# Time mixing: the next modulation tile's load is issued behind the present tile's instruction

## The chip, the cores and the metric

The kernel runs on one core of a Trainium2 chip. The metric is the device time of one execution in microseconds (us); lower is better. Before the change the median of three runs was 2669.53 us (2666.68 to 2670.61).

## What is computed

The reference is a two-layer encoder over 256 positions with 2048 channels. The first layer mixes along time with RWKV-7 recurrences for 32 heads, the second with chunked band attention; each layer ends in a squared-ReLU MLP. Cut to what matters here:

```
for layer in range(DEPTH):
    mod = c @ w_ada[layer] + b_ada[layer]
    sh1, sc1, gt1, sh2, sc2, gt2 = jnp.split(mod, 6, axis=-1)
    ...
    h = modulate(rms_norm(x, g_mix[layer]), sh1, sc1)
    y = rwkv7_time_mix(h, ...)          # layer 0; band attention in layer 1
    x = x + gt1[:, None, :] * y
    h = modulate(rms_norm(x, g_mlp[layer]), sh2, sc2)
    x = x + gt2[:, None, :] * sq_relu_mlp(h, w_up[layer], w_down[layer])
```

The **modulation** `mod` is a product of one row `c` with a matrix of 2048 x 12288 for each layer (and one of 2048 x 4096 for the shared keys and values). It has no use for TensorE's width, but all of its matrix must be read: it is cut into tiles of 128 x 1024, 384 of them behind the first two parts, 512 KB each. They are worked off in small steps beside the other work of the whole kernel.

## The kernel before

**Stages.** `layer_a` (L640) computes the first layer's projections up to v, and then the time mixing; `out_proj` (L929) follows, then the MLP, the attention, its `out_proj`, and the second MLP.

**The slots of the time mixing.** The heads are handled as 16 pairs. The loop at L896 runs over 8 x 16 + 36 = 164 slots. In each slot, every pair that is under way does one of its 36 steps (L907 to L910): `early` prepares its vectors, `invert` inverts a triangular matrix (on TensorE, L111, with VectorE's transposes L245 between), `late` runs the recurrence. A pair starts every 8 slots, the first at slot 8, with the matmuls L133 and L134. Behind these steps comes a slice of dense work (L921 to L923): in slots 0 to 127 two of the eight pieces of a projection (L860 to L870, `w_k` and `w_r` in turn, four slots each), afterwards pieces of the output projection `w_o` (`out_steps`, L872).

**Weights.** `weight` (L398) loads the two halves of a weight tile with `raw` (L366) and splits each in `halves` (L377): ScalarE casts it to wH (L384), VectorE subtracts to wL (L387). The load of the next projection's weight stands one projection ahead (`self.wnext`, L858). All loads are issued by SyncE (SP), in order, at L374 (parts of `w_o` at L395).

**Modulation.** `ada_tiles` (L433) lists the tiles, key by key, in two halves of sixteen. `ada_load` (L440) allocates a tile, issues its load and puts it in the queue `ada_q`. `ada_step` (L449) takes a tile from the queue, and calls `ada_load` first if the queue is empty; VectorE then adds the tile, times c, to `acc` (L460; the first of sixteen writes it, L458). Behind the sixteenth, `ada_sum` (L477) sums `acc` over the partitions with small matmuls (L482) and adds the bias (L486). `acc` has a single buffer, so the next sixteen begin when these matmuls have read it. `ada(n)` (L493) does n steps and then `ada_fill`, which loads ahead only where a stage has opened a pool of its own for these tiles (`ada_room`, tile `rada`). The time mixing has none: there `raw` takes the buffer from the six buffers of the tag `raw`, the same that the weights use. From slot 16 on, `self.ada()` is called in three slots of four (L924): 111 steps.

**What sets the order.** The code is traced in the order in which it stands; each engine's instructions are then ordered ahead of the run by a scheduler, which lets instructions that stand later go first where earlier ones are not ready. `issue_after(last)` keeps a block's matmuls behind the instruction `last` on TensorE. A load waits until the tile that had its buffer before has been read by its last reader.

**After the mixing.** `out_proj` loads x (L939), finishes the sums that `out_steps` began and, from n = 10 on, does one step for each tile that is still in the queue (`ada_drain`, L962). Today the queue is empty there.

Of the kernel before, what the change touches and what calls it, by code (L numbers as in the profile page):

```python
# [335 lines left out]
class Body:  # L336
# [303 lines left out]
    def layer_a(self, st, sp):  # L640
# [198 lines left out]
        with ExitStack() as s1:  # L839
            pw = self.pw = s1.enter_context(tc.tile_pool(name="pw", bufs=1, reuse_waits="tile"))  # L840
            pp = self.pp = sp.enter_context(tc.tile_pool(name="ps_b", bufs=1, space=bass.MemoryType.PSUM,
                                                         reuse_waits="tile"))
            self.psm = lambda: pp.tile([P, 512], F32, tag="ms", bufs=2, name="ms")
            self.bones = pw.tile([P, P], F32R, name="bones")
            nc.scalar.copy(self.bones, self.cst("bones"))
            e01 = [pw.tile([P, 4, C + 1], F32, name=f"e01_{i}") for i in range(2)]
            self.uf = [pw.tile([P, 4, C], F32, name=f"uf_{i}") for i in range(2)]
            for e, u in zip(e01, self.uf):
                nc.vector.memset(e[:, :, 0:1], 1.0)
                nc.gpsimd.memset(u, 0.0)  # L850

            pairs = [Pair(self, j, v[:, j, :], tw, ta, tg, e01[j % 2]) for j in range(NPAIR)]

            def proj_steps(pr):
                for dst, hl in (("k", xk), ("r", xr)):
                    w = self.wnext
                    src = next(weights, None)
                    self.wnext = None if src is None else self.weight(src)  # L858
                    ps = pp.tile([P, 2 * T], F32, tag="pj", bufs=2, name="pj")[:, :T]
                    for kt in range(KT):  # L860
                        self.proj(ps, w, lambda kt: hl[:, kt, :, 0:T], (kt, kt + 1))
                        if dst == "r" and kt == 1:
                            pr.lw = pw.tile([96, 2, P], F32, tag="lw", bufs=1, name="lw")
                            nc.sync.dma_start(out=pr.lw, in_=d["lora2"][pr.j, :96, 0:2])
                        if kt % 2 == 1:
                            if kt == KT - 1:
                                t = pw.tile([P, T], F32, tag=dst, bufs=2, name=dst)
                                nc.scalar.copy(t, ps)
                                setattr(pr, dst, t)
                            yield  # L870

            def out_steps():  # L872

                for n in range(8):
                    self.split(self.y_hl, n, v[:, n, :])
                sums, todo = self.o_ps, [(n, 0, HK) for n in range(8)] + [(n, HK, KT - 2) for n in range(4)]
                for n, lo, hi in todo:
                    if n % 2 == 0 and lo == 0:
                        tag = ("pj", "pj", "gr", "iv")[n // 2]
                        ps = pp.tile([P, 2 * T], F32, tag=tag, bufs=1 + (tag == "pj"), name="o")  # L880
                        sums.append(ps.rearrange("p (i t) -> p i t", i=2))
                    if lo == HK and n == 0:
                        assert all(p.done for p in pairs[:KT - 2])
                        for j in range(HK, KT - 2):
                            self.split(self.y_hl, j, v[:, j, :])
                    w = self.weight_part(d["w_o"][n], lo, hi)
                    for kt in range(lo, hi, 2):
                        self.proj(sums[n // 2][:, n % 2, :], w, lambda kt: self.y_hl[:, kt, :, 0:T],
                                  (kt, kt + 2), n % 2 == 0, False)
                        yield  # L890

            self.o_ps = []
            S, OUTS = self.SLOTS, 44
            inverts = range(Pair.EARLY, Pair.EARLY + Pair.INVERT)
            outs, done, n_out = None, 0, 0
            for slot in range(S * NPAIR + Pair.STEPS):  # L896
                live = []
                for j, pr in enumerate(pairs):
                    at = slot - S * (j + 1)
                    if 0 <= at < Pair.STEPS:  # L900
                        if at == 0:
                            pr.gen = pr.steps()
                        sums = at == Pair.STEPS - 3
                        live.append((0 if at in inverts else 1 + (at < Pair.EARLY) + 2 * sums, -at, pr))
                        pr.done = at == Pair.STEPS - 1
                last = self.last_pe()
                for _, _, pr in sorted(live, key=lambda x: x[:2]):  # L907
                    with tc.issue_after(last):
                        next(pr.gen)
                    last = self.last_pe()  # L910
                if slot < S * NPAIR:
                    if slot % S == 0:
                        dense = proj_steps(pairs[slot // S])
                    todo = 16 // S
                else:
                    if outs is None:
                        self.y_hl = self.new_hl()
                        outs = dense = out_steps()
                    todo = OUTS * (slot + 1 - S * NPAIR) // Pair.STEPS - n_out
                    n_out += todo  # L920
                with tc.issue_after(last):  # L921
                    for _ in range(todo):
                        next(dense, None)  # L923
                if slot >= 2 * S and slot % 4 < 3:  # L924
                    self.ada()
            self.fin(HK)
        return v

# [311 lines left out]
```

## Time and profile before

| | before |
|---|---|
| median of three runs | 2669.53 us (2666.68 to 2670.61) |
| profiled execution: its time | 2667.25 us |
| profiled execution: span | 2665.3 us |
| granted TensorE clock, mean | 0.992 |
| TensorE busy (matmul) | 2586.9 us, 97% |
| VectorE busy | 2104.5 us, 79% |
| ScalarE busy | 1369.2 us, 51% |
| moved by DMA | 662.69 MB, mean 249 GB/s |
| modulation loads: raw / rada from w_ada / rada from w_ada_kv | 111 / 209 / 64 |

How to read it: the span runs from the first to the last instruction of the core. PE is TensorE's matmuls and PEld its weight loads, which overlap; DVE is VectorE, ACT ScalarE, POOL GpSimd, SP SyncE, and a "q" behind an engine marks its sequencer (waits and issues of DMAs). A row of the timeline gives start, length, engine, line, operation, and the tile written and those read; in brackets the engine's idle time before it and what ended it. A row of waits gives the sum in us, how many times, and the longest. In rows by stretch, each engine's busy time is followed by its count of instructions.

### The profile page before, as it was taken

Reading aid. Unit: us, or ns where it says so; the run is one execution under the profiler, and the core shown is the slowest. Engines: PE = TensorE matmul, PEld = TensorE weight load, DVE = VectorE, ACT = ScalarE, POOL = GpSimd, SP = SyncE. Lnnn points to the kernel's source line nnn. Section 1 sums busy time; section 2 is a strip of 40 time slices with the busy share of each in tenths; the row PEclk is TensorE's granted clock in tenths of the full one; section 3 lists DMA queues with packets and bytes.
Section 4 is the critical chain, followed back from the end, with each engine's and each line's share of the span. In section 5 each row is a group of like instructions: output and inputs, shape, how many; then the busy total and the mean of one; then the engine's idle time right before and its main releaser. Section 6 shows DMA issues by size and latency. Waiting matters only on the chain.

```text
span 2665.3 us, 59286 instructions
## 1 busy us (share of the span) xinstructions
PE 2586.9 (97%) x24108; PEld 2258.5 (85%) x24108; DVE 2104.5 (79%) x3070; ACT 1369.2 (51%) x2516; POOL 210.2 (8%) x336
## 2 busy tenths in 40 slices
PE   7998999999999999999999999999999999999997
PEld 4788888888899888888888998877898888888886
DVE  6788888888889888888888898899887556556555
ACT  3345656556456345355365554565564464553554
POOL 0002323223100000000001100000100000000002
PEclk9999999999999999999999999999999999999999
DMA  9976656566768898889888779887766555555553
GB/s 353 313 243 205 202 183 201 182 202 199 252 235 308 309 324 323 318 328 335 319 328 292 231 248 322 320 274 256 267 215 237 185 188 189 184 188 190 189 190 119
DMA packets 207153, 662.69 MB, mean 249 GB/s; under 512 B 21408, under 2 KB 54560, under 8 KB 206880
## 3 DMA queue, kind: packets, MB, share of 16 engines
q1 hardware_dynamic: 204816, 656.36, 71.8%
q8 instruction: 189, 3.10, 0.5%
q10 hardware_dynamic: 2064, 2.54, 0.3%
q14 instruction: 84, 0.69, 0.1%
HBM read 656.72 MB, written 2.10 MB: 247 GB/s over the span
## 4 chain that ended last, share of the span: by engine, by line
PE 83%; DVE 7%; issue 3%; DMA 3%; ACT 2%; POOL 1%; DVEq 0%; ACTq 0%; SPq 0%; POOLq 0%
PE pj L418 41%; PE pj L419 21%; PE pj L407 3%; PE pj L408 3%; PE pj L409 3%; DVE wL L387 2%; DVE acc L460 2%; DMA raw<-w_ada 1%; PE iv L111 1%; DMA rada<-w_ada 1%; ACT wH L384 1%; PE o L407 1%; PE gr L105 1%; PE ms L330 1%; PE o L408 0%
## 5 line engine op out<-in xcount | busy, mean ns | idle before, releaser
L387 DVE TENSOR_TENSOR wL<-raw,wH 128x1024 fp32r<-128x1024 f32 x772 | 941.1, 1220 | 352.8 <-ACT wH L384 346.9
L384 ACT CAST wH<-raw 128x1024 fp32r<-128x1024 f32 x772 | 805.7, 1045 | 783.6 <-PE pj L418 594.6
L418 PE MATMUL pj<-aHL,wH 128*128 128x512 f32 x2816 | 998.1, 398 | 1.3 <-DVE x L953 1.3
L419 PE MATMUL pj<-aHL,wL 128*128 128x256 f32 x2816 | 791.4, 281 | 0.2 <-DVE wL L387 0.2
L418 PE MATMUL pj<-hHL,wH 128*128 128x512 f32 x2048 | 723.0, 398 | 0.0
L418 PEld LDWEIGHTS pj<-aHL,wH 128*128 128x128 f32 x2816 | 531.6, 189 | 129.4 <-issue 8.5
L419 PE MATMUL pj<-hHL,wL 128*128 128x256 f32 x2048 | 573.8, 280 | 0.3 <-DVE wL L387 0.3
L419 PEld LDWEIGHTS pj<-aHL,wL 128*128 128x128 f32 x2816 | 531.6, 189 | 1.8 <-issue 0.8
L418 PEld LDWEIGHTS pj<-hHL,wH 128*128 128x128 f32 x2048 | 384.7, 188 | 95.0 <-DVE hHL L999 0.2
L419 PEld LDWEIGHTS pj<-hHL,wL 128*128 128x128 f32 x2048 | 386.5, 189 | 0.8 <-DVE wL L387 0.6
L460 DVE SCALAR_TENSOR_TENSOR acc<-rada,ct,acc 128x1024 f32<-128x1024 f32 x256 | 328.2, 1282 | 11.1 <-DMA rada<-w_ada 10.1
L407 PE MATMUL pj<-aHL,wH 128*128 128x256 f32 (+1 forms) x896 | 263.3, 294 | 0.1
L408 PE MATMUL pj<-aHL,wH 128*128 128x256 f32 (+1 forms) x896 | 254.7, 284 | 0.0
L409 PE MATMUL pj<-aHL,wL 128*128 128x256 f32 (+1 forms) x896 | 253.5, 283 | 0.0
L524 POOL TENSOR_TENSOR ss<-ss,sq 128x256 f32<-128x256 f32 x56 | 54.1, 966 | 1588.2 <-ACT sq L523 1587.9
L407 PEld LDWEIGHTS pj<-aHL,wH 128*128 128x128 f32 x896 | 170.5, 190 | 5.1 <-issue 0.5
L409 PEld LDWEIGHTS pj<-aHL,wL 128*128 128x128 f32 x896 | 171.0, 191 | 0.2
L408 PEld LDWEIGHTS pj<-aHL,wH 128*128 128x128 f32 x896 | 170.6, 190 | 0.5
L1024 DVE SCALAR_TENSOR_TENSOR x<-pj,mod,x 128x256 f32<-128x256 f32 x256 | 123.4, 482 | 58.5 <-PE pj L419 54.9
L460 DVE SCALAR_TENSOR_TENSOR acc<-raw,ct,acc 128x1024 f32<-128x1024 f32 x104 | 139.9, 1345 | 12.9 <-DMA raw<-w_ada 12.3
L996 ACT ACTIVATE t<-t 128x256 f32<-128x256 f32 x112 | 46.8, 418 | 123.1 <-DVE t L968 123.1
L998 ACT ACTIVATE t<-t 128x256 f32<-128x256 f32 x128 | 53.4, 417 | 3.4
(250 smaller groups left out, 2825.3 us busy)
## 6 DMA issues: line engine op xcount, KB each, us to landing
raw<-w_up SPq DMA_DIRECT2D x256, 512.0 KB, 4.2
raw<-w_down SPq DMA_DIRECT2D x256, 512.0 KB, 4.3
rada<-w_ada SPq DMA_DIRECT2D x209, 512.0 KB, 5.8
raw<-w_ada SPq DMA_DIRECT2D x111, 512.0 KB, 4.4
rada<-w_ada_kv SPq DMA_DIRECT2D x64, 512.0 KB, 6.1
rawa<-w_ada SPq DMA_DIRECT2D x32, 512.0 KB, 6.8
rawa<-w_ada_t SPq DMA_DIRECT2D x32, 512.0 KB, 7.6
raw<-w_k SPq DMA_DIRECT2D x32, 512.0 KB, 3.9
```

Source lines behind the costliest of these rows:

```text
L384: nc.scalar.copy(Hf, raw)
L387: eng.tensor_tensor(out=Lf, in0=raw, in1=Hf, op=ALU.subtract)
L407: nc.tensor.matmul(ps, H[:, i, :], a(kt)[:, 0, :], start=(first and kt == 0), stop=False)
L408: nc.tensor.matmul(ps, H[:, i, :], a(kt)[:, 1, :], start=False, stop=False)
L409: ins = nc.tensor.matmul(ps, L[:, i, :], a(kt)[:, 0, :], start=False, stop=(last and kt == KT - 1))
L418: nc.tensor.matmul(ps, H[:, i, :], a(kt), start=(kt == 0), stop=False)
L419: ins = nc.tensor.matmul(ps[:, 0, :], L[:, i, :], a(kt)[:, 0, :], start=False, stop=(kt == KT - 1))
L460: nc.vector.scalar_tensor_tensor(out=self.acc, in0=raw, scalar=ck, in1=self.acc, op0=ALU.mult, op1=ALU.add)
L524: (eng or nc.gpsimd).tensor_tensor(out=self.ss, in0=self.ss, in1=sq, op=ALU.add)
L996: nc.scalar.activation(t, t, AF.Relu)
L998: nc.scalar.activation(t, t, AF.Square)
L1024: nc.vector.scalar_tensor_tensor(out=x, in0=ps[:, i, :], scalar=self.mods[(layer, 5)][:, n:n + 1], in1=x, op0=ALU.mult, op1=ALU.add)
```

## The change

In slots 16 and later with slot % 4 < 3 one step is still done. Behind it, and also in slot 15 and in every fourth slot, a tile is loaded if the queue is empty.

```
@@ -921,8 +921,11 @@
                 with tc.issue_after(last):
                     for _ in range(todo):
                         next(dense, None)
-                if slot >= 2 * S and slot % 4 < 3:
-                    self.ada()
+                if slot >= 2 * S - 1:
+                    if slot >= 2 * S and slot % 4 < 3:
+                        self.ada_step()
+                    if not self.ada_q:
+                        self.ada_load()
             self.fin(HK)
         return v
```

S is 8. The load of a step in slot 0, 1 or 2 of four then stands in the slot before, and for slot 0 two slots before, since the slot with remainder 3 does no step. The last step of the loop is that of slot 162; behind it the 112th tile is loaded, and its step is the first that `ada_drain` in `out_proj` finds.

## The prediction

> **What bounds the kernel now.** I read the page's head first, then busy time by stretch (the time mixing runs from 214 us, the first pair's matmul of L134, to 707 us, where the loads of x begin).
>
> ```profile
> span 2665.3 us, 59286 instructions
> ...
> PE 2586.9 (97%) x24108; PEld 2258.5 (85%) x24108; DVE 2104.5 (79%) x3070; ACT 1369.2 (51%) x2516; POOL 210.2 (8%) x336
> ```
> ```profile
> 214.00:707.00 493.00, 465.54 (x9965) 418.99 (x9964) 416.38 (x746) 278.99 (x787) 128.52 (x192) 0.99 0.63 200
> 707.00:760.00 53.00, 50.48 (x325) 46.34 (x324) 42.72 (x57) 29.95 (x49) 10.96 (x12) 0.97 0.86 287
> 760.00:2665.30 1905.30, 1888.28 (x12250) 1645.10 (x12249) 1482.51 (x1955) 973.80 (x1531) 55.90 (x111) 1.00 0.73 255
> ```
>
> The columns are PE, PEld, DVE, ACT and POOL, then clock, DMA share and GB/s. TensorE is the bound: outside the mixing it is idle for 17 us of 1905. In the mixing it is idle for 493.00 - 465.54 = 27.5 us; whatever the change can win there lies in these 27.5 us. VectorE is free for 493.00 - 416.38 = 76.6 us of the stage. Next, who TensorE waits for in that stretch, and everything that touches the tile "raw", which carries both the weights and the modulation:
>
> ```profile
> PE iv L111 <- DVE tt L245: 10.1, 11, 4.1
> ```
> ```profile
> L374 SPq DMA_DIRECT2D raw<-w_ada x111: 327/328/1397, 217.0 to 696.5; - x111
> L460 DVE SCALAR_TENSOR_TENSOR acc<-raw,ct,acc x104: 1236/1278/2173, 226.9 to 705.7; 128x1024 f32<-128x1024 f32 x104
> ...
>   PE pj L408: 43.6, 43
>   ACT wH L384: 15.5, 15
>   DMA raw<-w_ada: 12.3, 15
>   DMA raw<-w_o: 5.0, 2
> ```
>
> The largest wait of TensorE, 10.1 us, is on VectorE's transposes of the inversion. VectorE itself stands still for a modulation tile 15 times, 12.3 us in all; this is what the change aims at. The weights are early: the casts (wH, L384) wait for a matmul to free wH 43 times, never for a load of w_k or w_r, and for w_o twice (5.0 us).
>
> **When a load goes out today.** SP's queue and VectorE's releases of raw buffers, side by side (a row's x2 spans both issues, each 0.33 us long):
>
> ```profile
> 392.11 1.46 SPq L374 DMA_DIRECT2D raw<-w_k  x2
> 394.57 2.83 SPq L374 DMA_DIRECT2D raw<-w_ada  x2
> 398.67 0.33 SPq L864 DMA_DIRECT2D lw<-lora  x1
> 399.05 1.40 SPq L374 DMA_DIRECT2D raw<-w_ada  x1
> 402.71 2.31 SPq L374 DMA_DIRECT2D raw<-w_r  x2
> ```
> ```profile
> 390.79 1.28 DVE L460 SCALAR_TENSOR_TENSOR acc<-raw,ct,acc 128x1024 f32<-128x1024 f32 x1
> 392.00 1.22 DVE L387 TENSOR_TENSOR wL<-raw,wH 128x1024 fp32r<-128x1024 f32 x1
> 393.26 1.28 DVE L460 SCALAR_TENSOR_TENSOR acc<-raw,ct,acc 128x1024 f32<-128x1024 f32 x1
> 395.77 1.28 DVE L460 SCALAR_TENSOR_TENSOR acc<-raw,ct,acc 128x1024 f32<-128x1024 f32 x1
> ...
> 401.03 1.65 DVE L460 SCALAR_TENSOR_TENSOR acc<-raw,ct,acc 128x1024 f32<-128x1024 f32 x1 [1.48 <-DMA raw<-w_ada]
> ```
>
> The instruction at 390.79 ends at 392.07 and SP issues at 392.11; the next ends at 393.22, and the second w_k goes at 392.11 + 1.46 - 0.33 = 393.24; 394.54 is followed by 394.57, 397.05 by 397.07, 402.68 by 402.71. Each of these loads leaves within 0.04 us of a release. So all six raw buffers are always taken, and the hour of a load is set by the next buffer to come free, not by its place in the code. The step at 401.03 waits 1.48 us although SP issued its load the moment it could.
>
> How far do the steps already run ahead of their place in the code? Five rows: instructions of L460, of L458 and of L134 up to 401 us (the count stands behind the x), all of L134, and the last of L134 before it in the timeline.
>
> ```profile
> 200.00:401.00 201.00, 48.73 (x36) 0.98 0.63 198
> ```
> ```profile
> 200.00:401.00 201.00, 2.74 (x3) 0.98 0.63 198
> ```
> ```profile
> 200.00:401.00 201.00, 4.75 (x16) 3.04 (x16) 0.98 0.63 198
> ```
> ```profile
> L134 PE MATMUL ms<-ta,lw x32: 377/379/379, 214.3 to 627.0; 96*128 96x256 f32 x32
> ```
> ```profile
> 398.05 0.59 PE L134 MATMUL ms<-ta,lw 96*128 96x256 f32 x2
> ```
>
> Up to 401 us VectorE had begun 36 steps on L460 and 3 on L458 (the first of each sixteen), so the step at 401.03 is number 39, counted from 0. Three steps per four slots from slot 16 on put it at slot 16 + 4 x 13 = 68. L134 has two instructions for each pair: 32 of them, from 214.3 to 627.0, are 16 pairs in 412.7 us, so a pair's 8 slots take 412.7 / 15 = 27.5 us and a slot 3.44 us. The 16 up to 401 are eight pairs; the eighth begins in slot 64, at 398.05, and slot 68 comes at about 411.8. The step runs 11 us, three slots, before its place: it fills VectorE's gaps as soon as its tile has landed.
>
> **The change, part by part.** *The order of the loads.* Per four slots the old code asks SP for w, w, A, A, A, with each A (slots 0, 1, 2) just ahead of its own step. The new one asks in slot 0 for w, w, and behind each of the three steps for the next A: w, w, A, A, A again. What differs is one extra A at slot 15, ahead of the first w pair, and every A carries the tile one number on. Ring, releases and queue (SP's lw and lg among them) see the same sequence. The wait of 12.3 us therefore stays where it is, in front of another tile: 0 us. If I am wrong here, the bound is the 12.3 us less.
>
> A rule bears on this. The Trainium skill, "DMA: Bandwidth & Descriptors", section "Rules for kernel authors", says to issue a DMA early, compute, and wait late; by it the 12.3 us would go. The same skill, "Perfetto Trace Analysis", section "Identifying Performance Opportunities", says that a gap which repeats can mean that there is no SBUF for the next tile; by it this edit gives 0, and only a further buffer would help. The issue times above agree with the second.
>
> *One tile more in the ring.* One load (0.33 us of SP, 512 KB) and one step (1.28 us) come into the stage from the next one; 76.6 us of VectorE's idle time cover the step. At each sixteenth tile the steps stop until TensorE has summed the last sixteen:
>
> ```profile
> 361.30 1.27 DVE L460 SCALAR_TENSOR_TENSOR acc<-raw,ct,acc 128x1024 f32<-128x1024 f32 x1
> ...
> 377.51 0.74 DVE L458 TENSOR_SCALAR acc<-raw,ct 128x1024 f32<-128x1024 f32 x1
> ```
>
> During such a stop (16 us here) one A more is held, and the weights get their buffer one release later. A release comes 10 times in a pair's 27.5 us, so 2.75 us later; no cast waits for w_k or w_r today. 0 us, with 2.75 us for each of six stops if that cover were gone.
>
> *The end of the stage.* The load at slot 162 is of tile 111, whose step stands in the output projection (the drain at n = 10), where today nothing is left to drain. Its tile takes one of six buffers until VectorE gets to it.
>
> ```profile
> 699.31 8.48 SPq L395 DMA_DIRECT2D raw<-w_o  x7
> 707.89 6.82 SPq L939 DMA_DIRECT2D x<-x  x8
> ```
> ```profile
> 714.86 0.48 DVE L953 SCALAR_TENSOR_TENSOR x<-o,mod,x 128x256 f32<-128x256 f32 x1 [2.45 <-DMA x<-x]
> 715.26 1.22 DVE L387 TENSOR_TENSOR wL<-raw,wH 128x1024 fp32r<-128x1024 f32 x1
> ```
> ```profile
> 716.53 0.39 PE L409 MATMUL o<-aHL,wL 128*128 128x256 f32 x1 [2.52 <-DVE wL L387]
> ```
>
> Here the chain is bare: seven w_o loads wait for buffers on SP, x is queued behind them, VectorE waits 2.45 us for x with wL behind it, and TensorE 2.52 us for wL. The seven leave (8.48 - 0.33) / 6 = 1.36 us apart; with a buffer less, x is one release later: +1.4 us. It is 0 if the step runs before 707. I take +1.4, since the step's place is 30 us behind.
>
> *The next stage.* Tile 111 ends a sixteen, so tiles 112 to 115 are free of their sum earlier.
>
> ```profile
> L458 DVE TENSOR_SCALAR acc<-rada,ct x17: 743/745/748, 816.1 to 1980.8; 128x1024 f32<-128x1024 f32 x17
> ```
> ```profile
> 760.00:815.00 55.00, 55.00 (x420) 53.04 (x419) 48.33 (x84) 33.96 (x55) 2.10 (x3) 1.00 0.63 206
> ```
>
> Up to four steps, 4 x 1.28 = 5.1 us, move from 816 into a stretch with 6.7 us of VectorE free and TensorE full: 0 us, 5.1 us at worst. From there every step is one tick early; TensorE has no wait there to give or take.
>
> **Sum.** The profiled execution took 2667.25 us, 2.0 more than its span. 2667.25 + 0 + 0 + 1.4 + 0 = 2668.7. The median of the three runs is 2.3 above that execution; from it, 2669.5 + 1.4 = 2670.9. I say 2670.5.
>
> **The rivals.** *The early tile does help (faster).* For it: steps behind a pair of weight loads wait most, and a step with its tile already there would not. Against: the sequence w, w, A, A, A is unchanged. Its price: VectorE gets 12.3 us back, and at most the 10.1 us on the transposes reach TensorE; -10 us is 2659.5, half of it 2664.5. The overlap rule above is this rival.
>
> *Earlier steps get in the way (slower).* A step is 1.28 us that nothing interrupts, and the transpose tt (L245) of the inversion queues behind it on VectorE, iv on TensorE behind tt. With every tile there one turn sooner, just behind the stops at each sixteenth tile, more steps stand ahead of a tt. Price: the 10.1 us of that wait double, 2679.6. It decides from the point where more than half of a slot's steps come ahead of its tt. Against: number 39 is 11 us ahead already and TensorE loses only 27.5 us in all.
>
> *The weights late (slower).* The six stops at 2.75 us each are 16.5 us, 2686; unlikely, as only w_o's casts wait today.
>
> **How the numbers follow.** A measurement of this kernel can tell about 0.2%, 5.3 us. No change: 57%. The early tile helps: 19%, nearly all of it beyond 5.3 us. Steps in the way: 20%; weights late: 4%. Faster 0.19, same 0.57, slower 0.24. The range goes from the fastest run less the full wait, 2666.7 - 12.3 = 2654, to the slowest run with the transposes' wait doubled and the end's term, 2670.6 + 10.1 + 1.4 = 2682; the likeliest case alone lies in 2665 to 2676.
>
> **What would show it.** Right: SP's order in the mixing is still w, w, A, A, A with one A ahead; 112 loads of raw from w_ada and 208 of rada from w_ada; VectorE's wait for raw<-w_ada stays at 10 to 14 us; first to last L134 stays at 412.7 us within 3; the w_o loads near 707 issue about 1.4 us later. Wrong: that wait under 4 us with TensorE idle under 20 us (it helps), or iv waiting for tt over 15 us (in the way), or casts waiting for w_k or w_r.

## The result and the profile after

| | before | after |
|---|---|---|
| median, both run in turn on one chip (10 runs each) | 2665.86 us (2662.95 to 2673.17) | 2674.39 us (2668.97 to 2678.74) |
| ratio, 95% interval | | 1.0033 [1.0023, 1.0043] |
| second comparison: median | 2666.99 us | 2679.08 us |
| ratio, 95% interval | | 1.0040 [1.0026, 1.0055] |
| profiled execution: its time | 2667.25 us | 2673.63 us |
| profiled execution: span | 2665.3 us | 2671.8 us |

The change makes the kernel slower, by 0.33%: 8.5 us between the medians. That is inside the range that was given, but on the other side of the 0.2% bound: "no change", which had the largest chance, did not happen. One run of experiment 6 was a slow execution (4646.11 us, granted clock 0.842) and is left out of its median and its ratio.

**Where the time went.** First the head of the page of after, then line L418 in the two kernels. That line multiplies with wH wherever a projection is done as a whole: on `aHL` from the last eight tiles of the first output projection on, then in the attention's projections and the MLPs' way up; on `hHL` in the MLPs' way down. A row holds the count, the shortest/median/longest in ns, and the first and last start; the two kinds alternate.

```profile
span 2671.8 us, 59276 instructions
...
PE 2584.3 (97%) x24108; PEld 2259.2 (85%) x24108; DVE 2097.3 (78%) x3070; ACT 1371.3 (51%) x2516; POOL 213.4 (8%) x336
```

Before:

```profile
L418 PE MATMUL pj<-aHL,wH x2816: 387/396/504, 729.3 to 2559.4; 128*128 128x512 f32 x188
L418 PE MATMUL pj<-hHL,wH x2048: 389/398/500, 867.3 to 2649.8; 128*128 128x512 f32 x187
```

After:

```profile
L418 PE MATMUL pj<-aHL,wH x2816: 387/396/505, 733.3 to 2565.9; 128*128 128x512 f32 x188
L418 PE MATMUL pj<-hHL,wH x2048: 389/395/497, 878.9 to 2656.3; 128*128 128x512 f32 x187
```

The busy time of TensorE has not grown; it is the span that has. Up to the first L418, in the second half of the output projection, the profiled executions differ by 733.3 - 729.3 = 4.0 us. From there to the first matmul on `hHL` lie 867.3 - 729.3 = 138.0 us before and 878.9 - 733.3 = 145.6 us after: **7.6 us more, behind the edited loop: between the second half of the output projection and the first MLP's way down.** From there to the last matmul on `hHL`, after is faster again, 1777.4 us against 1782.5, but a second profile of the changed kernel (number 9) took 1781.1: that pace belongs to the execution (last section) and isn't the change.

The edited loop shows little. The loads of the mixing and what VectorE and TensorE wait for in it, after:

```profile
L374 SPq DMA_DIRECT2D rada<-w_ada x208: 327/328/1243, 747.4 to 2017.2; - x104
L374 SPq DMA_DIRECT2D raw<-w_ada x112: 327/328/1271, 212.0 to 703.8; - x112
```
```profile
DVE acc L460 <- DMA raw<-w_ada: 16.2, 17, 2.1
PE iv L111 <- DVE tt L245: 11.5, 10, 5.1
```

VectorE's wait for a modulation tile was 12.3 us in 15 waits and is 16.2 us in 17; the wait for the transposes was 10.1 us and is 11.5. Two timelines of SP's queue show what the edit did do. Before:

```profile
212.13 1.60 SPq L374 DMA_DIRECT2D raw<-w_r  x2
...
216.96 5.29 SPq L374 DMA_DIRECT2D raw<-w_ada  x3
```

After:

```profile
211.99 0.33 SPq L374 DMA_DIRECT2D raw<-w_ada  x1
213.28 0.33 SPq L374 DMA_DIRECT2D raw<-w_r  x1
...
217.82 5.47 SPq L374 DMA_DIRECT2D raw<-w_ada  x3
225.84 2.94 SPq L374 DMA_DIRECT2D raw<-w_k  x2
```

One modulation load is put ahead of the first `w_r`; from there it is two weights (the second `w_r` goes at 216.82), three modulation tiles, two weights, as before. One load was added at the front, and the whole sequence stands one place further back.

**The norm ahead of the first MLP.** The same stretch of VectorE's timeline in both, around the norm: the sum of squares is complete (L524), TensorE sums it over the partitions (L530), and rstd is made from it in L532 to L539 with two operations of ScalarE between. Everything that the way up gives on to the rest of the MLP passes through rstd. Before:

```profile
776.95 0.42 DVE L524 TENSOR_TENSOR ss<-ss,sq 128x256 f32<-128x256 f32 x1
...
780.76 0.42 DVE L537 SCALAR_TENSOR_TENSOR ru<-rstd 128x256 f32<-128x256 f32 x1 [0.93 <-ACT rstd L535]
...
781.68 0.43 DVE L539 SCALAR_TENSOR_TENSOR rstd<-ru,rstd 128x256 f32<-128x256 f32 x1
```

After:

```profile
775.65 1.29 DVE L460 SCALAR_TENSOR_TENSOR acc<-rada,ct,acc 128x1024 f32<-128x1024 f32 x1 [1.16 <-DMA rada<-w_ada]
...
785.11 0.41 DVE L524 TENSOR_TENSOR ss<-ss,sq 128x256 f32<-128x256 f32 x1
...
789.49 1.28 DVE L460 SCALAR_TENSOR_TENSOR acc<-rada,ct,acc 128x1024 f32<-128x1024 f32 x1 [2.42 <-DMA rada<-w_ada]
790.70 0.42 DVE L537 SCALAR_TENSOR_TENSOR ru<-rstd 128x256 f32<-128x256 f32 x1
791.07 1.28 DVE L460 SCALAR_TENSOR_TENSOR acc<-rada,ct,acc 128x1024 f32<-128x1024 f32 x1
792.27 0.42 DVE L538 TENSOR_TENSOR ru<-ru,rv 128x256 f32<-128x256 f32 x1
...
793.74 0.42 DVE L539 SCALAR_TENSOR_TENSOR rstd<-ru,rstd 128x256 f32<-128x256 f32 x1
```

From the start of the last L524 to the end of L539 it took 782.11 - 776.95 = 5.2 us before and 794.16 - 785.11 = 9.1 us after. Modulation steps stand between rstd's short operations now, and one of them waits 2.42 us for its tile, with L537 behind it, which reads no tile (VectorE takes its instructions in the order shown). Ahead of the norm there are three more such waits, 1.9 us together, 1.16 of them at 775.65. All four are one row of VectorE's waits from 725 to 830 us:

```profile
DVE acc L460 <- DMA rada<-w_ada: 4.3, 4, 2.4
```

No step was in this place before: there the first of these sixteen started at 816.1 us (the prediction's row for L458), here at 753.4. The sixteen are free this early because tile 111's sum (L482) runs at 718.4 us; before it ran at 815.2.

What TensorE waits for in this stretch, from 733 to 879 us, after; before, this view of its stretch has no row.

```profile
PE m L530 <- DVE ss L524: 2.7, 1, 2.7
PE pj L409 <- DVE wL L387: 1.7, 2, 0.9
PE pj L407 <- ACT wH L384: 1.4, 1, 1.4
```

These are 5.8 us. The rest, in this execution, is the clock. Three stretches of 3.4 us, in the columns of the prediction's view by stretch (clock third from the right):

```profile
782.40:785.80 3.40, 0.67 (x5) 0.47 (x5) 3.40 (x6) 1.75 (x3) 0.00 (x0) 1.00 0.75 273
785.80:789.20 3.40, 3.40 (x15) 3.23 (x15) 1.27 (x2) 1.02 (x3) 0.00 (x0) 0.50 0.89 290
789.20:792.60 3.40, 3.40 (x30) 3.40 (x30) 3.11 (x4) 1.41 (x2) 0.00 (x0) 1.00 1.01 388
```

In the second TensorE is busy throughout and starts 15 matmuls, in the third 30: at a granted clock of 0.50 the 3.4 us are worth 1.7. 5.8 + 1.7 = 7.5 us, which is the 7.6.

### The profile page after: what moved, and what is told of

It reads as the page before. It is cut to its first block, busy times and chain, and to the rows that moved or that the text cites. A ratio compares the mean times of both kernels' runs of the same rounds, so it can differ in the third digit from the quotient of the medians.

```text
span 2671.8 us, 59276 instructions
## 1 busy us (share of the span) xinstructions
PE 2584.3 (97%) x24108; PEld 2259.2 (85%) x24108; DVE 2097.3 (78%) x3070; ACT 1371.3 (51%) x2516; POOL 213.4 (8%) x336
## 4 chain that ended last, share of the span: by engine, by line
PE 80%; DVE 8%; issue 4%; DMA 4%; ACT 2%; POOL 1%; DVEq 0%; SPq 0%; ACTq 0%; POOLq 0%
PE pj L418 41%; PE pj L419 21%; PE pj L407 3%; PE pj L408 3%; PE pj L409 3%; DVE wL L387 2%; DVE acc L460 2%; DMA raw<-w_ada 2%; DMA rada<-w_ada 1%; PE iv L111 1%; PE gr L105 1%; ACT wH L384 1%; PE ms L330 1%; PE o L407 0%; PE pT L1131 0%
## 5 line engine op out<-in xcount | busy, mean ns | idle before, releaser
L418 PE MATMUL pj<-aHL,wH 128*128 128x512 f32 x2816 | 997.9, 398 | 1.1 <-DVE x L956 1.1
L418 PE MATMUL pj<-hHL,wH 128*128 128x512 f32 x2048 | 719.2, 396 | 0.0
L418 PEld LDWEIGHTS pj<-aHL,wH 128*128 128x128 f32 x2816 | 531.6, 189 | 128.8 <-issue 7.9
L418 PEld LDWEIGHTS pj<-hHL,wH 128*128 128x128 f32 x2048 | 384.0, 188 | 90.9 <-DVE hHL L1002 0.2
L460 DVE SCALAR_TENSOR_TENSOR acc<-rada,ct,acc 128x1024 f32<-128x1024 f32 x255 | 326.7, 1281 | 12.6 <-DMA rada<-w_ada 12.2
L524 POOL TENSOR_TENSOR ss<-ss,sq 128x256 f32<-128x256 f32 x56 | 55.1, 985 | 1591.4 <-ACT sq L523 1591.1
L460 DVE SCALAR_TENSOR_TENSOR acc<-raw,ct,acc 128x1024 f32<-128x1024 f32 x105 | 138.1, 1315 | 16.6 <-DMA raw<-w_ada 16.2
L999 ACT ACTIVATE t<-t 128x256 f32<-128x256 f32 x112 | 47.1, 420 | 126.9 <-DVE t L971 126.9
L1000 ACT ACTIVATE hHL<-t 128x256 fp32r<-128x256 f32 x128 | 53.0, 414 | 5.9 <-DVE t L572 5.0
```

Source lines behind the costliest of these rows:

```text
L418: nc.tensor.matmul(ps, H[:, i, :], a(kt), start=(kt == 0), stop=False)
L460: nc.vector.scalar_tensor_tensor(out=self.acc, in0=raw, scalar=ck, in1=self.acc, op0=ALU.mult, op1=ALU.add)
L524: (eng or nc.gpsimd).tensor_tensor(out=self.ss, in0=self.ss, in1=sq, op=ALU.add)
L999: nc.scalar.activation(t, t, AF.Relu)
L1000: nc.scalar.activation(h[:, 0, :], t, AF.Square)
```

## The experiments

Three theories were put to the test. **Theory N** (the norm): what costs is the 112th load alone. Tile 111 is the last of a sixteen; its step now stands in `out_proj`, its sum follows there, `acc` comes free, and the steps of the next sixteen fill VectorE's gaps while x is summed up and normalized, ahead of rstd. **Rival R** (the ring): what costs is the shifted order of loads in the mixing, with a modulation tile held in one of six buffers. **Rival L** (layout): any small edit of the order moves the time by as much. All ratios are against the kernel before, run in turn on the same chip; "the stretch" is from the first L418 on `aHL` to the first on `hHL`, 138.0 us before and 145.6 after.

**1. The changed kernel without the last load.**

```
-                    if not self.ada_q:
+                    if not self.ada_q and slot < 162:
                         self.ada_load()
```

> The changed kernel without the load behind the step of slot 162, so that 111 tiles are loaded and worked off in the time mixing, as before the change, and the output projection's drain finds nothing. Theory N (the loss at the first MLP's norm comes from tile 111's sum standing in the output projection, which lets the steps of tiles 112 on run there and stand ahead of the norm's rstd): the norm's stretch (729 to 867 us before) is as long as before, TensorE idle there 0 instead of 5.8 us; what stays is the 3 to 4 us of the mixing, ratio 1.000 to 1.002. Rival R (the earlier load costs it by what it does in the mixing and to the six raw buffers): ratio 1.003, as the changed kernel. Rival L (layout and order of the whole later program shift by chance): no forecast.

2668.02 us, 1.0002 [0.9993, 1.0011]. Its L418:

```profile
L418 PE MATMUL pj<-aHL,wH x2816: 388/396/505, 733.6 to 2562.7; 128*128 128x512 f32 x188
L418 PE MATMUL pj<-hHL,wH x2048: 389/398/501, 871.6 to 2653.1; 128*128 128x512 f32 x187
```

871.6 - 733.6 = 138.0 us: with one load of 112 gone, the loss behind the loop is gone.

**2. The kernel before, with that one step in `out_proj`.** All of the edited loop stays as it was.

```
                 elif n >= KT - 6:
+                    if begun and n == KT - 6:
+                        self.ada_step()
                     self.ada_drain(1)
```

> The kernel before, with one modulation step added in the first output projection at n = 10 (its load directly ahead of it); the time mixing is untouched. Theory N: +7 to +8 us over before (ratio 1.0025 to 1.003), TensorE idle 5 to 6 us between the end of the output projection and the first MLP's normed tiles, and a spell of 3.4 us at half clock behind that. Rival R: ratio 1.000, since no load in the mixing is early.

2674.03 us, 1.0030 [1.0020, 1.0041]. Its L418:

```profile
L418 PE MATMUL pj<-aHL,wH x2816: 388/396/504, 733.5 to 2570.8; 128*128 128x512 f32 x188
L418 PE MATMUL pj<-hHL,wH x2048: 389/398/500, 878.7 to 2659.7; 128*128 128x512 f32 x187
```

145.2 us. This one step, without any of the change, costs what the change costs. Its 7.2 us are made up a little differently: TensorE waits 6.2 us in the stretch, and no spell at half clock follows, though one had been forecast (the granted clock is 1.00 throughout); 1.0 us isn't placed. VectorE's waits for `rada` from 725 to 830 us are like those of after:

```profile
DVE acc L460 <- DMA rada<-w_ada: 5.5, 4, 2.3
```

**3. The changed kernel, with tile 111 left in the queue by `out_proj`.**

```
-                elif n >= KT - 6:
+                elif n >= KT - 6 and not begun:
                     self.ada_drain(1)
```

> The changed kernel without the drain in the first output projection, so that tile 111, loaded in slot 162, keeps its raw buffer until the first MLP's ticks. Theory N: no loss at the norm; ratio 1.000 to 1.002. Its raw ring is one buffer short through the whole output projection; if that were dear (the end-of-stage term of the prediction, 1.4 us) it shows between 700 and 760 us. Rival R: 1.003 or more.

2669.81 us, 1.0012 [1.0002, 1.0022]; the stretch is 875.6 - 737.6 = 138.0 us. All 112 loads are made in the mixing here; what is missing is only the step in `out_proj`, and so the sum.

**4. Another order in the mixing: the steps of the kernel before in other slots,** 111 as before.

```
-                if slot >= 2 * S and slot % 4 < 3:
+                if slot >= 2 * S - 1 and slot % 4 != 2 and slot < 163:
                     self.ada()
```

> The kernel before with its 111 steps in slots 15, 16, 17, 19, 20, 21 and so on (remainders 3, 0, 1) instead of 16, 17, 18, 20 (remainders 0, 1, 2); load and step stay together, as before. SP's order of loads in the mixing is then that of the changed kernel (one modulation load ahead of the first w_r pair). Theory N with 'the order of loads is all that the early load does': ratio 0.999 to 1.001, and no loss at the norm. Rival R, if the shifted order of loads itself costs: 1.002 to 1.003, with the mixing 3 to 4 us longer.

2670.84 us, 1.0009 [0.9998, 1.0019]; the stretch is 138.0 us. The wait for `raw<-w_ada` is 16.6 us in 17 waits: like that of after, in a kernel which loads nothing ahead. Neither L nor R gives 0.33%.

**5. The changed kernel, with all steps of the next sixteen behind rstd.** `rstd_ins` is the instruction of L539 of the norm before.

```
+            with self.tc.issue_after(self.rstd_ins) if key == (0, 5) and half else nullcontext():
                 nc.vector.tensor_scalar(out=self.acc, in0=raw, scalar1=ck, ...
```

> The changed kernel, whole, with one order added: the step of tile 112, and so every step behind it, stands behind the last VectorE instruction of the first MLP's rstd (L539). Tile 111's step and sum stay in the output projection, the early loads stay in the mixing. Theory N: the loss is made by the steps between 747 and 795 us, so it goes: ratio to before 1.000 to 1.001, TensorE idle at the norm 0 to 0.5 us. If instead the sum's matmuls in the output projection or the shift by one tile cost it: 1.003.

2669.88 us, 1.0018 [1.0006, 1.0029]; the stretch is 872.8 - 735.6 = 137.2 us, TensorE has no wait in it, and the first of the sixteen runs at 810.6 us. The loss in the norm is gone with the whole change in place. The ratio stays above 1, though, and a remainder is left for the mixing (below).

**6. The same, but only from the tenth step of the sixteen on** (tile 121); the nine ahead of it stay where the change put them.

```
+            with self.tc.issue_after(self.rstd_ins) if key == (0, 5) and half and kt == 9 else nullcontext():
                 nc.vector.scalar_tensor_tensor(out=self.acc, in0=raw, scalar=ck, in1=self.acc, ...
```

> The same order, but only from the tenth step of that sixteen on (tile 121, which ran at 789.5 us, ahead of rstd's last lines). The nine steps in the output projection's last third stay. If the steps inside the norm and their wait of 2.4 us for a load make the loss: ratio 1.000 to 1.001. If the nine steps before it, which make ss (L524) late, make it: TensorE still waits 2.7 us for ss and runs a spell at half clock (1.7 us), 4 to 5 us in all, ratio 1.0015 to 1.002.

2668.62 us, 1.0008 [0.9999, 1.0017]; the stretch is 875.5 - 737.3 = 138.2 us. The end of its norm on VectorE (two inserted lines shift the numbers: L462, L526, L539 and L541 are L460, L524, L537 and L539), and its modulation loads from 747 to 795 us with their median time to landing:

```profile
785.43 1.27 DVE L462 SCALAR_TENSOR_TENSOR acc<-rada,ct,acc 128x1024 f32<-128x1024 f32 x1
787.02 0.41 DVE L526 TENSOR_TENSOR ss<-ss,sq 128x256 f32<-128x256 f32 x1
...
789.83 0.42 DVE L539 SCALAR_TENSOR_TENSOR ru<-rstd 128x256 f32<-128x256 f32 x1 [0.93 <-ACT rstd L537]
...
790.75 0.43 DVE L541 SCALAR_TENSOR_TENSOR rstd<-ru,rstd 128x256 f32<-128x256 f32 x1
```
```profile
rada<-w_ada SPq DMA_DIRECT2D x14, 512.0 KB, 5.6
```

The same view of after, and of before:

```profile
rada<-w_ada SPq DMA_DIRECT2D x16, 512.0 KB, 6.1
```
```profile
rada<-w_ada SPq DMA_DIRECT2D x4, 512.0 KB, 6.4
```

This narrows N. Nine steps run ahead of the norm here too, and 14 loads go out instead of 4, and it costs TensorE one wait of 0.9 us. So the early steps as such and the traffic of their loads are a small part of the price. Two things are missing beside after: no step stands among the operations of rstd (by design), and none of the nine waited for its tile (in this execution; why its tiles were there in time isn't shown). Counted from the first L418 on `aHL`, the last addition to the sum of squares (L524, here L526) starts 776.95 - 729.3 = 47.7 us later in the kernel before, 787.02 - 737.3 = 49.7 here and 785.11 - 733.3 = 51.8 after: the nine steps alone make it 2.0 us later, the 1.9 us of waits for tiles about as much again, and the 2.7 us that TensorE waits on ss in after go with both. The 1.7 and 1.4 us that follow come behind the late rstd. ScalarE's casts of weights wait 3.8 us for a load there as well, and which of the two takes which part isn't separated.

**7. The kernel before, with the weights asked for half a projection later,** so that a modulation load stands nearer the front.

```
-                    self.wnext = None if src is None else self.weight(src)
                     ps = pp.tile([P, 2 * T], F32, tag="pj", bufs=2, name="pj")[:, :T]
                     for kt in range(KT):
+                        if kt == HK:
+                            self.wnext = None if src is None else self.weight(src)
```

> The kernel before, with the load and split of the next projection's weight (self.wnext) asked for in the middle of the present projection instead of at its start, two slots later; steps and loads of the modulation as before. If the six raw buffers set the hour of each load, fewer of them hold weights now and VectorE's wait for raw<-w_ada in the mixing falls from 12 to 16 us to under 6. If that wait costs TensorE time, the time falls by 3 to 8 us (ratio 0.997 to 0.999); if it lies in TensorE's shadow, 0.999 to 1.001. If the place of the load in the code set its hour, the wait stays at 12 to 16 us.

2668.81 us, 1.0003 [0.9991, 1.0014]. The wait for `raw<-w_ada` is 17.4 us in 14 waits: it didn't fall, though the forecast for buffers that set the hour was under 6 us. A row of VectorE and one of SP, from this kernel:

```profile
305.36 1.27 DVE L460 SCALAR_TENSOR_TENSOR acc<-raw,ct,acc 128x1024 f32<-128x1024 f32 x1
```
```profile
306.66 3.48 SPq L374 DMA_DIRECT2D raw<-w_k  x2
```

The step ends at 306.63, and the next load in the queue leaves at 306.66. The order was shifted, by two tiles this time, and a load still leaves at a release: so the forecast was wrong in what fewer waiting weights would do, not about the release. The kernel has 5 us more of that wait, and its interval ends at 1.0014, 3.7 us: part of the wait, at the least, does not reach TensorE.

**8. The kernel before, with the loads of x on GpSimd's queue,** past the `w_o` loads on SP: the end of the stage by itself.

```
                 if begun:
-                    nc.sync.dma_start(out=self.x[:, n, :], in_=d["x"][:, n, :])
+                    nc.gpsimd.dma_start(out=self.x[:, n, :], in_=d["x"][:, n, :])
```

> The kernel before, with the loads of x in the first output projection issued from GpSimd's queue in place of SP's, where they stand behind seven w_o loads that wait for raw buffers. The prediction's term for the end of the stage rests on that queue. If x is late because of SP's queue: VectorE's wait of 2.45 us for x at 714.9 us and TensorE's of 2.52 us go, and the half-clock spell behind it (3.4 us): 2 to 4 us less, ratio 0.9985 to 0.9993. If x waits for its space or the transfer itself, nothing: 1.000.

2665.34 us, 0.9993 [0.9984, 1.0002]. The load goes out at 705.34 us instead of 707.89, and VectorE's first step on x has no wait before it:

```profile
705.34 5.64 POOL L939 DMA_DIRECT2D x<-x  x10 [23.46 <-ACT sq L121]
```
```profile
712.68 0.88 DVE L953 SCALAR_TENSOR_TENSOR x<-o,mod,x 128x256 f32<-128x256 f32 x2
```

TensorE's wait of 2.52 us there is 1.1 us in two waits, from 700 to 745 us. The chain that the prediction read as bare at this place is one, but taking most of its wait away moves the median by less than its interval.

**9 to 11. Three kernels again: the changed one, number 1, number 8.**

> The changed kernel itself, beside the next run on one chip. Theory N: ratio 1.0025 to 1.004; in its profile the stretch from the output projection's last part to the 257th L418 matmul takes 144 to 146 us again (before 137.9), with VectorE waiting 3 to 5 us for rada loads ahead of rstd and a spell at half clock there. If that stretch was long by chance of one execution: under 140 us.

2679.08 us, 1.0040 [1.0026, 1.0055]. Its L418:

```profile
L418 PE MATMUL pj<-aHL,wH x2816: 388/396/504, 732.1 to 2571.1; 128*128 128x512 f32 x188
L418 PE MATMUL pj<-hHL,wH x2048: 389/398/498, 880.4 to 2661.5; 128*128 128x512 f32 x187
```

148.3 us, where 144 to 146 had been forecast; the step between rstd's operations again waits, 2.24 us. TensorE's waits in the stretch are 8.0 us, and 3.4 us run at a granted clock of 0.52, which costs 1.6: 9.6 us of the 10.3 more than before.

> The changed kernel without its last load, once more. Theory N: stretch 138 us; ratio as in its first run, 0.999 to 1.001; what it is above 1 is the cost of the shifted loads in the mixing. If the mixing costs the 3 to 4 us that the first profile of the changed kernel showed: 1.0012 to 1.0015.

2670.81 us, 1.0018 [1.0007, 1.0029]; the stretch is 872.4 - 734.4 = 138.0 us. The last load is worth 2679.08 - 2670.81 = 8.3 us in this comparison, where the two ran in turn, and by the ratios of their first runs 1.0033 - 1.0002 = 0.31%, again 8.3 us.

> The kernel before with x loaded from GpSimd's queue, once more, to narrow the interval of its first run (0.9984 to 1.0002). If that run's gain of about 2 us is real: ratio 0.9985 to 0.9998, and TensorE's wait behind x under 1.5 us again; if not, 1.000.

2664.98 us, 0.9993 [0.9982, 1.0004]; TensorE's wait behind x is 0.7 us.

**12. Numbers 5 and 8 together.**

> The changed kernel with both mends: the steps from tile 112 on behind rstd, and x from GpSimd's queue. If the changed kernel's early loads gain anything by themselves, it should beat the kernel before with x from GpSimd's queue (run beside it); Theory N says they gain nothing, so 0 to 0.15% above that one, and near 1.000 of the kernel before.

2666.33 us, 0.9994 [0.9984, 1.0004]; the stretch is 864.4 - 727.3 = 137.1 us. Beside number 11 (2664.98) the whole change, with its steps held behind the norm, is neither gain nor loss here.

**What stays open.** The kernels with the changed order in the mixing but without the loss in the norm (numbers 1, 3, 5, 6, 10) stand at 1.0002, 1.0012, 1.0018, 1.0008 and 1.0018: 0.12% on the mean, about 3 us, all on one side, and three of the five intervals (numbers 3, 5 and 10) exclude 1. But number 12 shows nothing of it, and number 1 and number 10 are the same kernel. Whether the shifted order costs 3 us or nothing isn't settled. The profiles lean towards a cost: from the first L134 to the last, the mixing takes 412.7 us on the mean in the four with its old order (before, 2, 8, 11: 411.2 to 414.1) and 415.3 in the eight with the new one (411.9 to 418.2). These ranges overlap, and number 7, at 419.5 us, is no slower in its time. A seventh buffer for `raw`, the direct test of the wait in the mixing, wasn't run. How much of the 0.33% the loss in the norm makes is known only roughly: holding the steps back in number 5 takes off 0.15%, leaving out the last load in number 1 takes off 0.31%. The best kernel found is number 8, 0.07% under before in both comparisons with 1 inside each interval: no gain that can be told.

## Why the prediction was right in its range and wrong in its mechanism, point by point

That the time lies in the range is luck. The range's upper end was made for the transposes of the mixing, and what cost the time had no term in the sum: it had +1.4 us, all at the end of the stage; measured are +8.5 us, with 7.6 us in the stretch that it put at 0. 2674.39 us even lies in the 2665 to 2676 of "no change", because the kernel before took 2665.86 us beside it and not the 2669.53 from which the forecast was made.

- **What bounds the mixing, and the order of the loads (0 us): right in the order, open in the 0 us.** The order on SP is w, w, A, A, A with one A more at the front, there are 112 loads of raw and 208 of rada, and the wait didn't fall. It left the 10 to 14 us that were named: 16.2 us in the profile and 15.2 in that of number 9. First to last L134 took 416.1 us, just outside the 3 us that were allowed, and 411.9 in number 9. Number 7 shows the reason given, the release of a buffer, in a second kernel. The overlap rule of the Trainium skill, "DMA: Bandwidth & Descriptors", "Rules for kernel authors", which would have taken the 12.3 us away, did not apply, since the loads were no earlier. In the changed kernel too they leave at a release: a step ends at 404.19 + 1.28 = 405.47 us, and the next w_r goes at 405.50.
- **One tile more in the ring (0 us): not contradicted.** No cast waits for w_k or w_r in the mixing of after. The open 3 us would belong here or to the order.
- **The end of the stage (+1.4 us): did not show as a wait.** Rows of after, first SP, then VectorE:

```profile
704.24 8.21 SPq L395 DMA_DIRECT2D raw<-w_o  x7
712.55 6.09 SPq L942 DMA_DIRECT2D x<-x  x8
```
```profile
710.82 1.28 DVE L460 SCALAR_TENSOR_TENSOR acc<-raw,ct,acc 128x1024 f32<-128x1024 f32 x1
...
718.78 0.48 DVE L956 SCALAR_TENSOR_TENSOR x<-o,mod,x 128x256 f32<-128x256 f32 x1 [1.89 <-DMA x<-x]
```

  Tile 111's step ran at 710.8 us, as a gap filler ahead of its place, just as number 39 had in the prediction. It ends at 712.10; the seventh w_o load leaves at 704.24 + 8.21 - 0.33 = 712.12 and x behind it, so x does hang on its buffer. But VectorE's wait for x is 1.89 us (2.45 before) and TensorE's behind it 1.33 (2.52): the rest of the stage had come later as well. The sign named for this term, w_o loads 1.4 us later, can't be read alone: they are 4.7 us later, and the last L134 is 3.3.
- **The next stage (0 us, at worst 5.1): this is the step of the prediction that failed.** The prediction said that "up to four steps" move into a stretch "with 6.7 us of VectorE free and TensorE full". It was mis-sized twice. With tile 111's sum done, not four tiles but the whole next sixteen are free, and 12 steps had begun by 794.1 us. And the price was taken as VectorE's busy time, a step's 1.28 us, against its free time. What a step costs is what stands behind it: 4.3 us of waiting for tiles, with the sum of squares and rstd behind the steps, TensorE behind these, and, in this execution, the half clock behind TensorE's gap: 7.6 us together. The prediction had seen that tile 111 ends a sixteen and that steps run ahead of their place; it asked whether VectorE had room for them and not which short chain they would stand in.
- **The rivals.** "Earlier steps get in the way" (20%) named the mechanism: a step that nothing interrupts, ahead of a short operation on VectorE for which TensorE waits. It put it at the transposes of the mixing, where the wait went from 10.1 us to 11.5 instead of doubling. It happened in the norm of the next stage, where the chain is as serial and a tile not yet landed makes the step longer. "The early tile helps" and "weights late" didn't occur.

## What to carry to other kernels

A load moved ahead in the code is no earlier while every buffer of its ring is taken: compare the hour of issue with the hour of release first. Where work is given out in small steps that fill gaps, an edit that shifts one of them over a limit (here the sum behind each sixteenth) frees a whole batch; look at which serial chain the batch then runs beside, above all a norm. And an operation that has to wait for its own tile costs its engine the wait on top of its own length: count it against whatever is queued behind it.

## What the runs showed of the hardware beyond this

**A short gap can cost more than itself.** Behind the gap of 2.73 us at TensorE (782.4 to 785.8 us, after) the granted clock is 0.50 for 3.4 us. The kernel before shows the same behind the wait of 2.52 us for wL at 716.5 us:

```profile
714.40:717.80 3.40, 1.27 (x10) 1.27 (x11) 2.94 (x6) 2.42 (x6) 0.00 (x0) 1.00 0.81 223
717.90:721.30 3.40, 3.40 (x18) 3.40 (x17) 3.40 (x6) 2.15 (x5) 3.16 (x3) 0.50 0.96 309
```

So each of these gaps cost about 1.7 us more. The length of a gap doesn't decide it alone. In the second profile of the changed kernel (number 9) the same wait on ss, 2.69 us at the same place, has full clock behind it; the half clock stands behind two shorter waits there, 1.37 and 0.93 us, at 803.4 and 804.8 us.

```profile
782.40:785.80 3.40, 0.71 (x6) 0.51 (x5) 3.40 (x6) 1.75 (x3) 0.00 (x0) 1.00 0.79 260
785.80:789.20 3.40, 3.40 (x26) 3.35 (x27) 1.42 (x2) 1.78 (x3) 0.00 (x0) 1.00 0.93 329
```

The Trainium skill, "TensorE: Matmul & The Clock Gate", "What's actually happening", has the clock halved after at least one idle window of about 3.4 us. The length of the spell agrees with that window; the gaps were shorter than it. Stretches of 3.4 us with TensorE busy for 0.67 and 1.27 us were followed by a spell, one with 0.71 us was not.

**One program, two paces.** Between its first matmul on `hHL` and the last, the changed kernel took 1777.4 us in its first profile and 2661.5 - 880.4 = 1781.1 in its second, with medians of 395 and 398 ns for one matmul. These 3.7 us belong to the execution and not to the edit; a difference of that size between two profiles has to be placed in a stretch before it is explained. The median alone doesn't tell it: numbers 8 and 11, one kernel too, have 398 and 396 ns and took 1781.7 and 1781.3 us.
